# Queries and keys of the dilated mixer as 2x2 block products: seven products for eight, in a written order

## The chip, the cores and the metric

The kernel runs on one core of one Trainium2 chip. The metric is the device time of one execution in microseconds (us), the median of several runs. Engines are named as in the profile: PE (TensorE, matmul), PEld (its weight loads), DVE (VectorE), ACT (ScalarE), POOL (GpSimd) and SP (SyncE, which here issues every DMA). L12 is line 12 of the kernel.

## The reference

One layer of an encoder over 1024 tokens of width 1024, in float32. The input is normalised and multiplied by one wide matrix, whose columns feed two attention mixers, their gates and a merge:

```python
h = rmsnorm(x, attn_norm_g)
proj = h @ w_in
(c_q, c_kv, k_rope, z_mla, q_dil, k_dil, v_dil, z_dil, g_mla, g_dil) = jnp.split(proj, ...)
a_out = mla_attention(c_q, c_kv, k_rope, ...)              # 8 heads, dense
y_mla = (a_out * silu(z_mla)) @ w_o_mla
d_out = dilated_mixture(q_dil, k_dil, v_dil, positions)    # 24 heads of 64
y_dil = (d_out * silu(z_dil)) @ w_o_dil
merged = sigmoid(g_mla + b) * y_mla + sigmoid(g_dil + b) * y_dil
return x + merged @ w_out                                  # and a last rmsnorm
```

`dilated_mixture` applies rope (a rotation of the two halves of each head by cosine and sine tables) to `q_dil` and `k_dil`, then lets three groups g = 0, 1, 2 of 8 heads attend in windows with dilation 1, 4 and 16. The change concerns `q_dil` and `k_dil`: h times 3072 of the columns of `w_in`, then rope.

## The kernel before

**Numbers.** Every product is float32 out of three fast matmuls: an operand x is split into a high part (a cast by ACT, L75) and a low part x - high (a subtraction by POOL or DVE, L76), and `mm3` (L67 to L71) adds high·high, high·low and low·high in PSUM. The normalised input lies transposed in SBUF as hT_h and hT_l (8 blocks of 128 rows by 1024 tokens); its factor per token, R, is multiplied in later (for queries and keys it is folded into the rope tables cs_d).

**Stages on PE.** First the latent projections, the latents of mixer A and the dilated values (`dil_v`, six calls, one for each group g and half "quad" of its heads), to 229.6 us. Then `dil_qk` (L371 to L404), 12 items: for quad 0 and 1, for g = 0, 1, 2, for q and k. Then dilated attention (`dil_attention`, L724), dense attention (`mla_attention`, L499), and `output` (L796).

**One item of `dil_qk`.** It loads two weight tiles of 1024 x 128 (`wtile`, L79: load w_raw, cast w_h on ACT, subtract w_l on POOL), a for the first halves of four heads, b for the second. For each half of the tokens it makes two PSUM tiles, pa and pb, of 8 row blocks x 3 matmuls, 128x512 each: 96 matmuls an item. `rope` (L226) makes four DVE products out of each pair (L233), POOL subtracts and adds (L234, L235). For g < 2 the result is split again (ACT, POOL) into dq_st; for g = 2 ACT copies it in another token order (L397). The result goes to HBM (s_dq, s_dk) in DMAs of 32 rows, 128 KB each, from where attention loads it head by head: op_b the queries, op_a the keys, op_c the values.

**What sets the order.** The Tile scheduler orders every engine's instructions from the program, its dependences and its own estimates; pools of SBUF and PSUM tiles set when a tile may be written again. In the six-buffer PSUM pool pj of this stage, PE can work ahead of DVE. All DMAs go through SP's queue in order, so that one that waits holds up those behind it.

**At the stage's end.** `run` opens the PSUM pools of attention and starts `fillers` (L415): the 32 projections for z and the gates, 24 matmuls of 128x512 each half, that are fed between attention's steps (`feed`, L55). FIRST_FEED = 19 steps go ahead of the first scores (s_ps, L634). Scores pass `soft_block` (L603: on DVE L607, which needs the masks, on ACT L608). The masks are loaded into a pool that takes over SBUF from dil_qk's tiles. Attention's op tiles lie in SBUF that is free during `dil_qk`, and the first two heads' loads are issued inside that stage.

Of the kernel before, what the change touches and what calls it, by code (L numbers as in the profile page):

```python
# [39 lines left out]


# [8 lines left out]
class Net:  # L50
# [16 lines left out]
    def mm3(self, out, lh, ll, rh, rl, start, stop):  # L67
        mm = self.nc.tensor.matmul
        mm(out, lh, rh, start=start, stop=False)  # L69
        mm(out, lh, rl, start=False, stop=False)  # L70
        return mm(out, ll, rh, start=False, stop=stop)  # L71
# [7 lines left out]
    def wtile(self, src, wp=None, n=8):  # L79
        raw = self.wp.tile([128, 8, 128], F32, name="w_raw")  # L80
        wp = wp or self.wp
        h = wp.tile([128, 8, 128], F32R, name="w_h")
        l = wp.tile([128, 8, 128], F32R, name="w_l")
        self.dma(raw[:, :n], src)
        self.split(raw[:, :n], h[:, :n], l[:, :n], self.nc.gpsimd)
        return h, l

    def proj_half(self, w, half, pool):

        return run_all(self.proj_steps(w, half, pool))  # L90

    def proj_steps(self, w, half, pool):
# [3 lines left out]
        for kc in range(8):  # L96
            self.mm3(ps, w[0][:, kc], w[1][:, kc], self.hTh[:, kc, t], self.hTl[:, kc, t], kc == 0, kc == 7)
            if kc < 7:
                yield
# [235 lines left out]
    def dil_v(self, g, quad, tp, pj):  # L335
# [3 lines left out]
        for kk in range(2):  # L339
            raw = self.wp.tile([128, 4, 256], F32, name="w_raw")  # L340
            wp = (self.wp, self.wpx)[kk]
            h = wp.tile([128, 4, 256], F32R, name="w_h")
            l = wp.tile([128, 4, 256], F32R, name="w_l")
            self.dma(raw, a["wv"][g * 2 + quad, kk])
            self.split(raw, h, l, nc.gpsimd)
            w.append((h, l))
        for t in range(8):
            ps = pj.tile([128, 512], F32, name="pj")[:, :256]
            for kc in range(8):
                wh, wl = w[kc // 4]  # L350
                sl = slice(128 * t, 128 * t + 128)
                self.mm3(ps, self.hTh[:, kc, sl], self.hTl[:, kc, sl], wh[:, kc % 4], wl[:, kc % 4], kc == 0, kc == 7)
# [18 lines left out]
    def dil_qk(self, g, quad, which, tp, pj):  # L371

        nc, a = self.nc, self.a
        base = T_QK + (g * 2 + quad) * 4 + which * 2
        wa, wb = self.wtile(a["wt"][base]), self.wtile(a["wt"][base + 1], wp=self.wpx)
        if g < 2:
            st = [[tp.tile([128, S], F32R, name=f"dq_st{c}{p}") for p in range(2)] for c in range(2)]
        else:
            st = [[tp.tile([128, S], F32, name=f"dq_st{c}0")] for c in range(2)]
        for half in range(2):  # L380
            c512 = slice(half * 512, half * 512 + 512)
            pa, pb = self.proj_half(wa, half, pj), self.proj_half(wb, half, pj)
            o = self.rope(pa, pb, self.cos_d[:, c512], self.sin_d[:, c512], tp)
            for c in range(2):
                if g == 0:
                    self.split(o[c], st[c][0][:, c512], st[c][1][:, c512], nc.gpsimd)
                    continue
                if g == 1:
                    src = o[c].rearrange("p (m r) -> p r m", r=4)
                    dst = [x.rearrange("p (r m) -> p r m", r=4)[:, :, 128 * half:128 * half + 128] for x in st[c]]  # L390
                    self.split(src, dst[0], dst[1], nc.gpsimd)
                else:

                    src = o[c].rearrange("p (m b e) -> p e b m", b=8, e=2)
                    dst = st[c][0].rearrange("p (e b m) -> p e b m", e=2, b=8)[:, :, :, 32 * half:32 * half + 32]
                    for e in range(2):
                        nc.scalar.copy(out=dst[:, e], in_=src[:, e])  # L397
        off = 64 if (g == 0 and which) else 0
        dst = (self.dq if which == 0 else self.dk)[g]
        for c in range(2):  # L400
# [619 lines left out]
```

## Time and profile before

| what | value |
| --- | --- |
| runs | 1333.28, 1333.55, 1335.28 us; median 1333.55 |
| profiled execution | 1340.99 us, of which the span is 1339.2 us |
| granted PE clock, mean | 0.983 |
| values, latents (PE) | to 229.6 us |
| `dil_qk` (PE) | 229.67 to 490.9 us |
| dilated attention | about 498 to 835 us |
| dense attention | about 835 to 1200 us |
| output | to the end |

The profile counts from the start of the span. A row of groups reads: line, engine, operation, what is written <- what is read (names without buffer numbers), partitions x elements, how often | busy us, mean ns of one | idle time of the engine ahead of it, and who ended it. A timeline row starts with the start and the length in us; in brackets stands how long the engine was idle before and who ended that. "DMA to landing" is the time from issue to arrival.

### The profile page before, as it was taken

Reading aid. Unit: us, or ns where it says so; the run is one execution under the profiler, and the core shown is the slowest. Engines: PE = TensorE matmul, PEld = TensorE weight load, DVE = VectorE, ACT = ScalarE, POOL = GpSimd, SP = SyncE. Lnnn points to the kernel's source line nnn. Section 1 sums busy time; section 2 is a strip of 40 time slices with the busy share of each in tenths; the row PEclk is TensorE's granted clock in tenths of the full one; section 3 lists DMA queues with packets and bytes.
Section 4 is the critical chain, followed back from the end, with each engine's and each line's share of the span. In section 5 each row is a group of like instructions: output and inputs, shape, how many; then the busy total and the mean of one; then the engine's idle time right before and its main releaser. Section 6 shows DMA issues by size and latency. Waiting matters only on the chain.

```text
span 1339.2 us, 19315 instructions
## 1 busy us (share of the span) xinstructions
PE 1275.4 (95%) x7101; PEld 1108.4 (83%) x7101; DVE 655.4 (49%) x1204; ACT 563.3 (42%) x1102; POOL 455.0 (34%) x302
## 2 busy tenths in 40 slices
PE   8989999999999999988989889999999999998998
PEld 8879999888888878877878777788888878886786
DVE  7483520222222224656576565656555556558622
ACT  6533332123322225545455453455554545444322
POOL 2251212576466634525422031212111022035522
PEclk9989999999999999989999999999999999999999
DMA  9747562585345535678777778545333463136322
GB/s 322 227 154 272 196 248 80 162 217 159 106 115 151 135 98 164 163 184 224 190 186 208 196 195 203 156 120 160 92 99 100 103 178 119 63 116 205 131 96 75
DMA packets 128253, 213.03 MB, mean 159 GB/s; under 512 B 36440, under 2 KB 65696, under 8 KB 126304
## 3 DMA queue, kind: packets, MB, share of 16 engines
q1 hardware_dynamic: 128160, 211.81, 54.6%
q8 instruction: 56, 0.92, 0.3%
q14 instruction: 37, 0.30, 0.1%
HBM read 143.01 MB, written 68.75 MB: 158 GB/s over the span
## 4 chain that ended last, share of the span: by engine, by line
PE 70%; DMA 9%; DVE 5%; issue 2%; SPq 1%; ACT 1%; POOL 1%; DVEq 0%; ACTq 0%; POOLq 0%
PE pj L69 17%; PE pj L70 16%; PE pj L71 16%; PE pt L543 4%; PE av L552 2%; PE av L551 2%; PE s_mla L69 2%; PE s_mla L71 2%; PE s_mla L70 2%; DMA s_sd<-av_t 2%; PE pt L642 2%; SPq L65 1%; PE av L663 1%; DMA op_a<-s_dk 1%; PE s_ps L698 1%
## 5 line engine op out<-in xcount | busy, mean ns | idle before, releaser
L69 PE MATMUL pj<-hT_h,w_h 128*128 128x512 f32 x768 | 315.0, 410 | 3.7 <-DVE zg_z L428 2.1
L76 POOL TENSOR_TENSOR w_l<-w_raw,w_h 128x1024 fp32r<-128x1024 f32 (+1 forms) x70 | 167.5, 2396 | 441.1 <-ACT w_h L75 371.4
L71 PE MATMUL pj<-hT_h,w_l 128*128 128x512 f32 x768 | 301.9, 393 | 0.0
L70 PE MATMUL pj<-hT_l,w_h 128*128 128x512 f32 x768 | 301.6, 393 | 0.0
L233 DVE TENSOR_TENSOR rope_m<-pj,cs_d 128x512 f32<-128x512 f32 x96 | 61.9, 686 | 241.1 <-PE pj L71 241.1
L76 DVE TENSOR_TENSOR pt_l<-pt,pt_h 128x512 fp32r<-128x512 f32 x192 | 131.6, 686 | 89.0 <-ACT pt_h L75 87.1
L71 PEld LDWEIGHTS pj<-hT_h,w_l 128*128 128x128 f32 x768 | 145.3, 189 | 31.5
L69 PEld LDWEIGHTS pj<-hT_h,w_h 128*128 128x128 f32 x768 | 145.8, 190 | 29.7 <-DVE zg_z L428 3.0
L75 ACT CAST pt_h<-pt 128x512 fp32r<-128x512 f32 x192 | 112.0, 584 | 130.0 <-PE pt L543 60.0
L70 PEld LDWEIGHTS pj<-hT_l,w_h 128*128 128x128 f32 x768 | 146.0, 190 | 24.4
L70 PE MATMUL pj<-w_l,hT_h 128*128 128x256 f32 x384 | 109.6, 286 | 0.0
L71 PE MATMUL pj<-w_h,hT_l 128*128 128x256 f32 x384 | 109.4, 285 | 0.0
L69 PE MATMUL pj<-w_h,hT_h 128*128 128x256 f32 x384 | 109.3, 285 | 0.0
L75 ACT CAST w_h<-w_raw 128x1024 fp32r<-128x1024 f32 (+1 forms) x70 | 72.3, 1034 | 74.5 <-PE pj L70 59.5
L529 DVE TENSOR_REDUCE m_nm<-s_mla 128x1 f32<-128x1024 f32 x64 | 78.0, 1221 | 32.6 <-PE s_mla L71 32.4
L608 ACT ACTIVATE p<-p,d_st 128x256 f32<-128x256 f32 x128 | 64.4, 505 | 60.5 <-DVE d_st L607 60.4
L532 ACT ACTIVATE p<-s_mla,m_nm 128x1024 f32<-128x1024 f32 x64 | 71.8, 1123 | 25.5 <-PE pt L543 19.2
L543 PE MATMUL pt<-consts,p 128*128 128x128 f32 x512 | 79.6, 276 | 0.0
L552 PE MATMUL av<-pt_l,op_c 128*128 128x256 f32 x256 | 67.2, 286 | 8.5 <-DVE pt_l L76 8.5
L69 PEld LDWEIGHTS pj<-w_h,hT_h 128*128 128x128 f32 x384 | 73.6, 192 | 1.1
L607 DVE CUSTOM_DVE_ANT_0 p<-s_ps,masks 128x256 f32<-128x256 f32 x128 | 51.0, 417 | 48.0 <-PE s_ps L635 27.3
L70 PEld LDWEIGHTS pj<-w_l,hT_h 128*128 128x128 f32 x384 | 73.7, 192 | 0.7
(232 smaller groups left out, 2548.4 us busy)
## 6 DMA issues: line engine op xcount, KB each, us to landing
w_raw<-wt SPq DMA_DIRECT2D x48, 512.0 KB, 4.7
op_b<-s_dq SPq DMA_DIRECT2D x32, 512.0 KB, 8.5
s_dq<-dq_st SPq DMA_DIRECT2D x80, 128.0 KB, 2.6
s_dk<-dq_st SPq DMA_DIRECT2D x80, 128.0 KB, 2.4
gate<-s_gt SPq DMA_DIRECT2D x34, 256.0 KB, 3.0
s_dv<-dv_st SPq DMA_DIRECT2D x32, 256.0 KB, 3.9
s_gt<-zg_t SPq DMA_DIRECT2D x32, 256.0 KB, 3.7
w_raw<-wv SPq DMA_DIRECT2D x12, 512.0 KB, 5.9
```

The source lines that it names most:

```text
L69: mm(out, lh, rh, start=start, stop=False)
L70: mm(out, lh, rl, start=False, stop=False)
L71: return mm(out, ll, rh, start=False, stop=stop)
L75: self.nc.scalar.copy(out=h, in_=raw)
L76: sub.tensor_tensor(out=l, in0=raw, in1=h.bitcast(F32), op=ALU.subtract)
L233: v.tensor_tensor(out=mi, in0=p, in1=tab, op=ALU.mult)
L529: v.tensor_reduce(out=nm[:, hh, qb:qb + 1], in_=s, axis=AX.X, op=ALU.max, negate=True)
L532: nc.scalar.activation(out=p, in_=s, func=AF.Exp, bias=nm[:, hh, qb:qb + 1], accum_out=den[:, hh, qb:qb + 1])
L543: self.anchor = nc.tensor.transpose(pt[:, o:o + 128], P[b2][:, 128 * kc:128 * kc + 128], self.ident)
L552: nc.tensor.matmul(a_out, vv[:, kc], pl[:, s], start=False, stop=kc == 7)
L607: nc.vector.tensor_tensor_reduce(out=p, in0=s, in1=mask, op0=ALU.add, op1=ALU.min, scale=-0.125, scalar=3e38, accum_out=nm)
L608: nc.scalar.activation(out=p, in_=p, func=AF.Exp, scale=-1.0, bias=nm, accum_out=den)
```

## The change

`dil_qk` goes. An item is now computed as a product of 2x2 blocks in seven block products in place of eight (Strassen's method in Winograd's form). The weights' blocks are a or b by the upper or lower 512 rows; the activations' blocks are the first or second 512 tokens by the same rows. Each block product is 4 row blocks x 3 matmuls, 128x512.

- The activations' four sums (s0 to s3, high and low, 64 KB a partition) are made once (`block_sums`), beside the last four `dil_v`: x^T is loaded again, scaled on ACT, summed on POOL, split on ACT and DVE.
- Per item POOL makes four differences of weight blocks (`block_minus`) and the seven operands' low parts (`block_operand`), five places (LEAD) ahead of their products.
- The products gather in four PSUM banks a, b, c, d, of two sets in turn, so that all eight banks are used. ACT copies three of them, DVE adds these in place, and rope follows in place: sines into SBUF, cosines in the bank, then the difference and the sum, which POOL did before.
- All of this stands under `manual_schedule`: `blocks` writes the order of each engine, place by place.

```diff
+    def block_minus(self, j, items):
+        n, k = divmod(j, 7)
+        if n < len(items) and k in (2, 3, 4, 6):
+            b = self.blk[n]
+            out, x, y = {2: ((0, 0), (0, 1), (0, 0)), 3: ((0, 1), (1, 1), (0, 1)), 4: ((0, 0), (1, 1), (0, 0)), 6: ((1, 0), (1, 0), (0, 0))}[k]
+            self.nc.gpsimd.tensor_tensor(out=b[out], in0=b[x], in1=b[y], op=ALU.subtract)
...
+    def block_product(self, j, ps):
+        k = j % 7
+        hx = lambda i, c: tuple(x[:, 4 * c:4 * c + 4, 512 * i:512 * i + 512] for x in (self.hTh, self.hTl))
+        act = (lambda: hx(0, 0), lambda: hx(0, 1), lambda: self.s[0], lambda: self.s[2], lambda: self.s[1], lambda: self.s[3], lambda: hx(1, 1))[k]()
+        w = self.opd.pop(j)
+        out = ps["abcdacd"[k]]
+        for kc in range(4):
+            self.mm3(out, w[0][:, kc], w[1][:, kc], act[0][:, kc], act[1][:, kc], k < 4 and kc == 0, k in (1, 4, 5, 6) and kc == 3, skip=True)
...
+        steps = {
+            2: [lambda: copied(0, a)],
+            3: [lambda: add(b, 0)],
+            4: [lambda: copied(1, c)],
+            5: [both],
+            6: [lambda: copied(2, a), lambda: add(a, "t")],
+            7: [lambda: add(c, 2)],
+            9: [lambda: add(d, 2)],
+        }
...
+        r0, r1 = rope(0, b, c), rope(1, d, a)
+        put(7, r0[0])
+        put(8, r0[1])
+        put(8, r0[2])
+        put(9, r1[0])
+        put(10, lambda: high(0, (b, c)))
+        put(10, r1[1])
+        put(11, r1[2])
+        put(11, lambda: low(0, (b, c)))
+        put(12, lambda: high(1, (d, a)))
+        put(12, lambda: store(0))
+        put(12, lambda: low(1, (d, a)))
+        put(13, lambda: store(1))
...
+        with self.tc.manual_schedule():
+            for x in range(1, places + 14):
+                n, k = divmod(x - 1, 7)
+                j = x - 1
+                if j < places:
...
+                    self.block_product(j, ps[n])
+                todo = []
+                for m, y in ((n, k + 1), (n - 1, k + 8)):
+                    if m in steps:
+                        todo += steps[m].pop(y, [])
+                for f in todo:
+                    f()
+                self.block_operand(j + LEAD, items)
+                self.block_minus(j + LEAD + 1, items)
+                if k == 2 and n + 2 < len(items):
+                    self.block_loads(n + 2, items[n + 2])
```

Three edits go with it. **Stores by tile:** an item of g = 0 is stored in 4 DMAs, of g = 1 in 8, of g = 2 in 2, in place of 16, 16 and 8; s_dq and s_dk are laid out in HBM by quad and row for it. Attention then loads a head's keys in two DMAs, not one, and for g = 2 queries and keys in eight, not four. **Waits by bytes:** every pool gets `reuse_waits="tile"`, so that a tile waits for those tiles alone whose bytes it takes over. **Weights in pieces:** `wtile` and `dil_v` split weights in halves, each with tiles of its own.

```diff
-        self.dma(k[:, :S + pad], self.dk[g][h].rearrange("a c r t -> (a c r) t"))
+        for p in range(2):
+            self.dma(k[64 * p:64 * p + 64, :S + pad], self.dk[g][h // 4][:, hr, p])
...
-            with tc.tile_pool(name="op", bufs=1) as self.op, tc.tile_pool(name="ap", bufs=1) as ap:
+            with tc.tile_pool(name="op", reuse_waits="tile", bufs=1) as self.op, tc.tile_pool(name="ap", reuse_waits="tile", bufs=1) as ap:
```

How instructions stand is shown at three places. The first is DVE in the middle of the stage. Before (pj are the PSUM tiles pa and pb of one half, L233 rope's products):

```order
L233 TENSOR_TENSOR rope_m1_4257<-pj_4231,cs_d_544 128x512
L233 TENSOR_TENSOR rope_m2_4258<-pj_4231,cs_d_544 128x512
L233 TENSOR_TENSOR rope_m0_4320<-pj_4270,cs_d_544 128x512
L233 TENSOR_TENSOR rope_m3_4323<-pj_4270,cs_d_544 128x512
L233 TENSOR_TENSOR rope_m1_4321<-pj_4295,cs_d_544 128x512
L233 TENSOR_TENSOR rope_m2_4322<-pj_4295,cs_d_544 128x512
```

Now (st_a0 to st_d0 are one item's banks, st_a1 to st_d1 the next one's; st_c and st_t are SBUF copies; L450 and L451 combine, L483 to L491 are rope, L514 is the low part):

```order
L514 TENSOR_TENSOR dq_st00_3196<-st_b0_2968,dq_st00_3196 128x512
L514 TENSOR_TENSOR dq_st10_3197<-st_c0_2969,dq_st10_3197 128x512
L450 TENSOR_TENSOR st_t_3245<-st_d1_3138,st_c_3222 128x512
L514 TENSOR_TENSOR dq_st01_3247<-st_d0_2970,dq_st01_3247 128x512
L514 TENSOR_TENSOR dq_st11_3248<-st_a0_2967,dq_st11_3248 128x512
L451 TENSOR_TENSOR st_a1_3135<-st_a1_3135,st_t_3245 128x512
L451 TENSOR_TENSOR st_c1_3137<-st_c1_3137,st_c_3274 128x512
L483 TENSOR_TENSOR rope_m0_3299<-st_c1_3137,cs_d_543 128x512
L483 TENSOR_TENSOR rope_m1_3301<-st_b1_3136,cs_d_543 128x512
L487 TENSOR_TENSOR st_b1_3136<-st_b1_3136,cs_d_543 128x512
L487 TENSOR_TENSOR st_c1_3137<-st_c1_3137,cs_d_543 128x512
L490 TENSOR_TENSOR st_b1_3136<-st_b1_3136,rope_m0_3299 128x512
```

Where DVE only multiplied out of PSUM, it now combines, rotates and splits, with the ends of one item between the beginnings of the next, and many rows write the bank that they read.

The second place is DVE at the hand-over to attention. Before, the last rope products are followed by the first filler's z (L428) and the first soft_block (L607):

```order
L233 TENSOR_TENSOR rope_m1_4321<-pj_4295,cs_d_544 128x512
L233 TENSOR_TENSOR rope_m2_4322<-pj_4295,cs_d_544 128x512
L428 TENSOR_TENSOR zg_z_4386<-pj_4361,R_95 128x512
L607 ISA p_4469,d_st_4459<-s_ps_4468,masks_4453 128x256
L607 ISA d_st_4459 128x1
```

Now the same z (L601) and soft_block (L780) stand behind what the last product leaves to do:

```order
L451 TENSOR_TENSOR st_d1_4486<-st_d1_4486,st_c_4598 128x512
L483 TENSOR_TENSOR rope_m0_4625<-st_a1_4483,cs_d_543 128x512
L483 TENSOR_TENSOR rope_m1_4627<-st_d1_4486,cs_d_543 128x512
L487 TENSOR_TENSOR st_d1_4486<-st_d1_4486,cs_d_543 128x512
L487 TENSOR_TENSOR st_a1_4483<-st_a1_4483,cs_d_543 128x512
L490 TENSOR_TENSOR st_d1_4486<-st_d1_4486,rope_m0_4625 128x512
L491 TENSOR_TENSOR st_a1_4483<-st_a1_4483,rope_m1_4627 128x512
L601 TENSOR_TENSOR zg_z_4695<-pj_4670,R_95 128x512
L780 ISA p_4783,d_st_4772<-s_ps_4782,masks_4766 128x256
```

Seven operations on the last bank and its neighbour now stand between the last product and z, where two stood.

The third place is SP's queue around the masks' load. Before (s_dk_67 are the last item's stores; the first heads' loads of op_a, op_b and op_c stand some 60 rows earlier):

```order
L65 DMA s_dq_64<-dq_st_4055 32x1024 x4
L65 DMA w_raw<-wt 128x1024
L65 DMA s_dk_67<-dq_st_4204 32x1024 x4
L65 DMA s_dk_67<-dq_st_4205 32x1024 x4
L65 DMA masks<-masks 128x1280
```

Now:

```order
L67 DMA s_dq_64<-dq_st_4545 128x1024
L67 DMA op_b<-s_dq_62 64x1x2048 x2
L67 DMA op_a<-s_dk_65 64x1x1152 x2
L67 DMA op_c<-s_dv_68 128x9x128
L67 DMA op_b<-s_dq_62 64x1x2048 x2
L67 DMA op_a<-s_dk_65 64x1x1152 x2
L67 DMA op_c<-s_dv_68 128x9x128
L67 DMA w_raw<-wt 128x1024
L67 DMA s_dk_67<-dq_st_4629 128x1024
L67 DMA s_dk_67<-dq_st_4630 128x1024
L67 DMA masks<-masks 128x1280
```

The first two heads' loads have come behind the stage, between the last two items' stores: their SBUF is that of the sums.

More of the change, by code (lines that the diff above doesn't have):

```diff
@@ new lines, in run @@
+                            self.dil_v(0, 1, vp, pj)
+                    sp = sums.enter_context(tc.tile_pool(name="sums", reuse_waits="tile", bufs=1))
+                    with tc.tile_pool(name="bs", reuse_waits="tile", bufs=1) as tp:
+                        self.block_sums(sp, tp)
+                        self.dil_v(1, 0, vp, pj)
+                    for g, quad in ((1, 1), (2, 0), (2, 1)):
+                        self.dil_v(g, quad, vp, pj)
+                    for x in (self.cos_d, self.sin_d):
+                        for half in range(2):
+                            c = slice(512 * half, 512 * half + 512)
+                            nc.gpsimd.tensor_tensor(out=x[:, c], in0=x[:, c], in1=self.R[:, c], op=ALU.mult)
@@ L946, in run @@
             at.close()
-            with tc.tile_pool(name="yo", bufs=5, space=PSUM) as py:
+            with tc.tile_pool(name="yo", reuse_waits="tile", bufs=5, space=PSUM) as py:
                 self.output(py)
```

259 lines of the change are left out of this document (173 added, 86 removed).

## The prediction

> **What bounds the kernel now.** I read the page from the top: busy shares, the chain, the costliest groups.
>
> ```profile
> span 1339.2 us, 19315 instructions
> PE 1275.4 (95%) x7101; PEld 1108.4 (83%) x7101; DVE 655.4 (49%) x1204; ACT 563.3 (42%) x1102; POOL 455.0 (34%) x302
> PE 70%; DMA 9%; DVE 5%; issue 2%; SPq 1%; ACT 1%; POOL 1%; DVEq 0%; ACTq 0%; POOLq 0%
> L69 PE MATMUL pj<-hT_h,w_h 128*128 128x512 f32 x768 | 315.0, 410 | 3.7 <-DVE zg_z L428 2.1
> ```
>
> TensorE (PE) is busy for 95% of the span, so a matmul that goes is worth its pitch wherever PE never waits. Whether that holds in the changed stage is read from that stage's own windows. The columns are the stretch, its length, then busy time of PE, PEld, DVE, ACT and POOL with instructions, the granted clock, DMA share and GB/s:
>
> ```profile
> 250.00:300.00 50.00, 50.00 (x223) 41.39 (x221) 11.60 (x18) 12.35 (x14) 34.26 (x23) 1.00 0.75 206
> 300.00:350.00 50.00, 50.00 (x222) 41.42 (x221) 11.99 (x19) 14.60 (x17) 29.64 (x19) 1.00 0.57 155
> 350.00:400.00 50.00, 50.00 (x223) 41.39 (x222) 12.50 (x20) 13.76 (x19) 30.25 (x21) 1.00 0.38 106
> 400.00:450.00 50.00, 50.00 (x222) 41.42 (x221) 11.60 (x18) 13.62 (x14) 34.85 (x23) 1.00 0.50 137
> ```
>
> PE has no gap and the full clock; DVE is a quarter busy, ACT a quarter, POOL two thirds. So PE alone paces this stage, and the other engines have room, POOL least. The pitch is 200 us by 890 matmuls = 0.225 us. The whole stage gives it more exactly. These are its first and last matmul in the timeline, and the first of the next stage:
>
> ```profile
> 229.67 0.40 PE L69 MATMUL pj<-hT_h,w_h 128*128 128x512 f32 x1
> ...
> 490.62 0.39 PE L71 MATMUL pj<-hT_h,w_l 128*128 128x512 f32 x1
> ...
> 492.48 0.47 PE L69 MATMUL pj<-hT_h,w_h 128*128 128x512 f32 x1 [1.47 <-DVE rope_m L233]
> ```
>
> With 12 items of 96 matmuls, 1152 in all, that is 260.95 us over 1151 gaps = 0.2267 us.
>
> **What goes.** Seven products of 4 row blocks and 3 matmuls are 84 per item: 1008 in place of 1152, of the same form. 144 x 0.2267 = **32.6 us**, if PE stays the pace. An item then has 19.0 us, a product (a "place") 2.72 us.
>
> **What the other engines must do in 19.0 us.** Grouped rows of the stage, forms apart:
>
> ```profile
> L233 DVE TENSOR_TENSOR rope_m<-pj,cs_d 128x512 f32<-128x512 f32 x94 | 60.6, 686 | 237.1 <-PE pj L71 237.1
> L76 POOL TENSOR_TENSOR w_l<-w_raw,w_h 128x1024 fp32r<-128x1024 f32 x24 | 57.5, 2396 | 32.3 <-DMA s_dv<-dv_s 18.3 <-ACT w_h L75 14.1
> L76 POOL TENSOR_TENSOR dq_st<-rope_m,dq_st 128x512 fp32r<-128x512 f32 x32 | 45.0, 1431 | 0.0
> L235 POOL TENSOR_TENSOR rope_m<-rope_m,rope_m 128x512 f32<-128x512 f32 x23 | 29.8, 1295 | 0.0
> L75 ACT CAST dq_st<-rope_m 128x512 fp32r<-128x512 f32 x32 | 27.9, 872 | 91.7 <-POOL rope_m L234 53.9 <-POOL rope_m L235 24.5 <-DMA s_dk<-dq_st 6.6
> L75 ACT CAST w_h<-w_raw 128x1024 fp32r<-128x1024 f32 x23 | 24.3, 1055 | 54.3 <-PE pj L70 54.3
> L397 ACT COPY dq_st<-rope_m 128x256 f32<-128x256 f32 x28 | 16.6, 640 | 41.4 <-POOL rope_m L234 36.3 <-POOL rope_m L235 4.8
> L76 DVE TENSOR_TENSOR pt_l<-pt,pt_h 128x512 fp32r<-128x512 f32 x192 | 131.6, 686 | 89.0 <-ACT pt_h L75 87.1
> L75 ACT CAST pt_h<-pt 128x512 fp32r<-128x512 f32 x192 | 112.0, 584 | 130.0 <-PE pt L543 60.0
> ```
>
> *DVE*: 5 combines, 12 of rope, 4 low parts (none for g=2): 21 x 0.686 = 14.4 us, 76%. Each reads one PSUM and one SBUF operand, as the two DVE rows do. New is that most write their PSUM bank in place, which no row shows. I take 0.686 because inputs, shape and type are those of these rows; below, back to back, the pairs of L233 run at 0.645 (1.29 us for two). The point at which DVE takes over the pace is 19.0/21 = 0.905 us.
>
> *POOL*: 7 low parts of 128x512 at half of 2396 and 4 differences at 1.295 = 13.6 us; all eleven at 1.431 are 15.7 us, 83%. It takes over at 19.0/11 = 1.73 us.
>
> *ACT*: 3 copies out of PSUM at 0.584, 7 casts at half of 1055, 4 high parts at 0.872 (or 8 at 0.640): 8.9 to 10.6 us.
>
> So operands, made five places (13.6 us) ahead, and combines, with two places (5.4 us) until the item after next wants the bank, hide behind the products. If POOL or DVE ran 10% over 19.0 us, the stage would cost 12 x 1.9 = 23 us more. Rope's sums leave POOL for DVE; that is counted above. Stores fall from 160 to 56 DMAs; they lie under the products in both.
>
> The row that could speak against DVE at 0.686 is a DVE subtraction with both operands in SBUF, against L233 under the same busy POOL (min/median/max ns):
>
> ```profile
> L76 DVE TENSOR_TENSOR mg_l<-gate,m x16: 678/1251/1783, 1216.1 to 1254.3; 128x512 fp32r<-128x512 f32 x16
> L233 DVE TENSOR_TENSOR rope_m<-pj,cs_d x96: 680/688/694, 235.4 to 491.7; 128x512 f32<-128x512 f32 x96
> ```
>
> With two SBUF inputs the same shape stretches to 1251; with one in PSUM it never exceeds 694. The combines are of the second kind, so I keep 0.686. [...]
>
> **The block sums** are new: 16 reloads of x^T, 16 ACT scalings, 16 POOL sums, 16 splits (ACT cast, DVE subtract). SP issues the reloads behind the last latents' stores and the first two stores of the fifth group of values, so some 40 us of value products (16 tiles of 24 matmuls at 0.12 us, less two tiles) still lie over them.
>
> ```profile
> 229.43 0.28 PE L70 MATMUL pj<-w_l,hT_h 128*128 128x256 f32 x1
> 229.55 0.28 PE L71 MATMUL pj<-w_h,hT_l 128*128 128x256 f32 x1
> w_raw<-wt SPq DMA_DIRECT2D x48, 512.0 KB, 4.7
> ```
>
> POOL needs 16 x 1.295 + 8 x 1.25 = 31 us, DVE 16 x 1.251 = 20 us beside it; the third product, the first that reads a sum, comes 5.4 us later still. About 14 us spare. The loads of item 1's weights, though, stand on SP behind a load for item 2, which waits for POOL's last operand of item 0, some 8 us into the stage; they land at 8 + 4.7, and POOL must then make an operand by 19 us. That fits, with POOL behind. For both I take **+1 us**, from 0 to 8.
>
> **The hand-over to attention** is where something comes back. T0 is the end of the last product (before: 490.62 + 0.23 = 490.85).
>
> ```profile
> 491.05 1.29 DVE L233 TENSOR_TENSOR rope_m<-pj,cs_d 128x512 f32<-128x512 f32 x2 [4.05 <-PE pj L71]
> ...
> 494.40 3.58 SPq L65 DMA_DIRECT2D s_dk<-dq_st  x8
> ...
> 500.27 0.35 SPq L65 DMA_DIRECT2D masks<-masks  x1
> ...
> 505.33 0.08 DVE L607 DVE_READ_ACCUMULATOR2_ANT d_st<- 128x1 f32 x1
> ...
> 505.47 0.39 PE L634 MATMUL s_ps<-op_a,op_b 128*128 128x256 f32 x1 [0.74 <-DVE d_st L607]
> ```
> ```profile
> DMA to landing us min/median/max: 3.9/3.9/3.9
> ```
>
> (The last row is the mask load's.) Before, soft_block waits for the masks, the masks for the last s_dk stores, whose SBUF they take; PE goes on at T0 + 14.6. After: DVE's 14 operations since the last but one product (7 from T0 - 2.7, 7 from T0) end at T0 + 6.5, ACT's four half copies at T0 + 9.1, two store issues (0.45 each) at T0 + 10, the masks' issue 2.3 later as before, landing 3.9 later, the first soft_block 0.8 and s_ps 0.5 behind: T0 + 17.5, **+2.9 us**. Meanwhile the scores' banks are the last item's accumulators: PE has 24 filler matmuls (to T0 + 5.4) and then stands 3.7 us until ACT has copied. In before PE stood 1.5 there. What so long a gap does is seen at a load wait:
>
> ```profile
> 574.00:578.60 4.60, 0.53 (x3) 0.13 (x1) 1.06 (x2) 1.29 (x3) 2.52 (x2) 0.92 1.04 261
> 578.60:580.00 1.40, 1.26 (x6) 1.29 (x7) 0.46 (x3) 0.00 (x0) 0.00 (x0) 0.50 0.99 205
> 584.00:588.00 4.00, 4.00 (x12) 3.23 (x12) 1.48 (x3) 0.31 (x1) 0.00 (x0) 0.50 0.84 254
> 588.00:592.00 4.00, 4.00 (x24) 3.42 (x23) 2.60 (x11) 2.24 (x9) 0.00 (x0) 0.98 0.21 16
> ```
>
> After some 4 us without matmuls the granted clock is 0.50 for about 9 us, which loses 4.7 us of work. At the hand-over PE must do 8 score and 24 filler matmuls (1 + 5.4 us) from T0 + 9.1: done at T0 + 15.5 at full clock, at T0 + 20.2 with those 4.7 us. So the hand-over costs from +2.9 to +5.6 us; I take **+4.3**. [...]
>
> The first two heads' loads, issued under the stage before, now wait for the sums' SBUF and start about T0 - 5 (the second sum's product is over at T0 - 5.4): 2.2 MB a head at 261 GB/s are 8.4 us, landed at T0 + 3.5, before the scores.
>
> **Elsewhere** keys come in two loads, class loads in eight, at 0.45 us of SP each; waits go by bytes. PE's waits that this touches, and the one it could shorten:
>
> ```profile
> PE pj L69 <- DVE gate L825: 5.3, 4, 2.1
> PE s_ps L634 <- DMA op_b<-s_dq: 4.2, 1, 4.2
> PE s_ps L634 <- DMA op_a<-s_dk: 3.3, 1, 3.3
> ```
>
> 12.8 us in all: from -5 to +8, taken as 0, since loads get later by a few issues and releases earlier.
>
> **The sum.** -32.6 + 1 + 4.3 = -27.3 us. The profiled execution took 1340.99 us (span 1339.2), so it would take 1313.7. It is 7.4 us over the median of the runs, 1333.55, at the same instructions; the stage ran at full clock there, so the difference carries over: **1306.2 us**. With both ends of the terms: 1333.55 - 32.6 + (0 to 8) + (2.9 to 5.6) + (-5 to +8) = 1298.9 to 1322.6.
>
> **Rivals.**
> - *DVE or POOL paces the stage, slower than before.* Place: DVE's in-place operations. It decides from 0.905 us an operation; the whole gain is gone when an item takes 19.0 + 27.3/12 = 21.3 us, at 1.01 us. With the 1.251 of the row with two SBUF inputs, 12 x (26.3 - 19.0) = 88 us less the 27.3: about 1394 us. For it: writes to PSUM by DVE are unseen. Against: 680 to 694 ns at PSUM inputs, under a POOL as busy as it will be. 7%.
> - *The hand-over or the start is dearer*: scores that wait for heads' loads crowded with the stores, item 1's weights late, sums late: 8 to 15 us more than taken, as a load wait with its half clock costs (4.2 + 4.7 us each): 1314 to 1322. For it: ten loads move from under the stage to its end. 15%.
> - *Waits by bytes gain besides*: the output stage's gate waits and head loads shorten by 5 to 9 us of those 12.8: 1297 to 1301. Against: most of these waits are for loads, not for releases. 8%.
> - *The gain is given back* in attention, by queues on SP that now hold more loads ahead of PE: within 2.7 us of 1333.55. It would take three more such load waits. 3%.
>
> **How the numbers follow.** The forecast holds 67%. Low 1297 takes in the third rival, high 1322 the second: some 88% by these cases, and I leave it so wide for what a new order in attention may do. A difference of 0.2% (2.7 us) is about what a measurement tells from none: faster 0.89, same 0.04, slower 0.07.
>
> **What would show it.** Right: 1008 block matmuls at 0.227 us without gaps, a stage near 229 us, DVE about 75% and POOL about 72 to 83% busy there, DVE operations near 0.69; a PE stop near 3.7 us after the first filler product, scores going on about T0 + 18 to 20. Wrong: PE waiting on w_l, st or sums inside the stage; in-place DVE operations over 0.9 us; attention longer by more than 8 us.

## The result

The changed kernel takes **1735.68 us** (median of 4 runs, 1733.21 to 1739.72) against 1333.41 us for the kernel before in the same comparison: a ratio of **1.3011, 95% interval 1.2978 to 1.3043**. It is slower by 30%, where the prediction had 1306.2 us in a range of 1297 to 1322 and gave "slower" 7 in 100. In the comparisons below one run of the version that loads the second head later took 4692.85 us and one of the kernel before 1400.65; the ratios leave both out, and their cause is not known.

### The profile page after: what moved, and what is told of

Read it like the earlier page. It is cut to its first block, busy times and chain, and to the rows that moved or that the text cites. A ratio compares the mean times of both kernels' runs of the same rounds, so it can differ in the third digit from the quotient of the medians.

```text
span 1733.7 us, 19520 instructions
## 1 busy us (share of the span) xinstructions
PE 1274.6 (74%) x6957; PEld 1105.9 (64%) x6957; DVE 752.8 (43%) x1359; ACT 610.6 (35%) x1276; POOL 498.5 (29%) x393
## 4 chain that ended last, share of the span: by engine, by line
PE 50%; DMA 29%; SPq 9%; DVE 6%; issue 3%; ACT 2%; POOL 1%; ACTq 0%; DVEq 0%; POOLq 0%
DMA op_a<-s_dk 13%; SPq L67 9%; PE pj L71 7%; PE pj L73 7%; PE pj L72 7%; DMA op_b<-s_dq 3%; PE pt L716 3%; DMA s_sd<-av_t 3%; DMA s_rr<-c_w 2%; PE av L725 2%; PE av L724 2%; PE s_mla L71 1%; PE s_mla L73 1%; PE s_mla L72 1%; PE st_a L73 1%
## 5 line engine op out<-in xcount | busy, mean ns | idle before, releaser
L78 POOL TENSOR_TENSOR w_l<-w_raw,w_h 128x512 fp32r<-128x512 f32 (+1 forms) x176 | 233.3, 1333 | 630.0 <-ACT w_h L77 534.6
L809 PE MATMUL s_ps<-op_a,op_b 128*128 128x256 f32 x128 | 47.2, 377 | 405.3 <-DMA op_a<-s_dk 244.4
L780 DVE CUSTOM_DVE_ANT_0 p<-s_ps,masks 128x256 f32<-128x256 f32 x128 | 51.8, 417 | 397.5 <-PE s_ps L810 273.5
L71 PE MATMUL pj<-hT_h,w_h 128*128 128x512 f32 x384 | 171.7, 447 | 1.9 <-DVE zg_z L601 1.9
L72 PE MATMUL pj<-hT_l,w_h 128*128 128x512 f32 x384 | 157.0, 409 | 0.0
L73 PE MATMUL pj<-hT_h,w_l 128*128 128x512 f32 x384 | 156.2, 407 | 0.0
L77 ACT CAST w_h<-w_raw 128x512 fp32r<-128x512 f32 (+1 forms) x176 | 106.0, 614 | 127.8 <-POOL w_raw L415 65.4
L73 PEld LDWEIGHTS pj<-hT_h,w_l 128*128 128x128 f32 x384 | 76.2, 198 | 17.8
L71 PEld LDWEIGHTS pj<-hT_h,w_h 128*128 128x128 f32 x384 | 77.7, 202 | 12.9 <-DVE zg_z L601 2.5
L72 PEld LDWEIGHTS pj<-hT_l,w_h 128*128 128x128 f32 x384 | 77.8, 203 | 10.3
L73 PEld LDWEIGHTS pj<-w_h,hT_l 128*128 128x128 f32 x384 | 73.4, 191 | 0.9
```

What stands on the lines that cost most here:

```text
L71: mm(out, lh, rh, start=start, stop=False, skip_group_check=skip)
L72: mm(out, lh, rl, start=False, stop=False, skip_group_check=skip)
L73: return mm(out, ll, rh, start=False, stop=stop, skip_group_check=skip)
L77: self.nc.scalar.copy(out=h, in_=raw)
L78: sub.tensor_tensor(out=l, in0=raw, in1=h.bitcast(F32), op=ALU.subtract)
L780: nc.vector.tensor_tensor_reduce(out=p, in0=s, in1=mask, op0=ALU.add, op1=ALU.min, scale=-0.125, scalar=3e38, accum_out=nm)
```

## The profile after

The page of the changed kernel: span, busy time, the granted clock in 40 slices, and the group with the longest idle time before it.

```profile
span 1733.7 us, 19520 instructions
PE 1274.6 (74%) x6957; PEld 1105.9 (64%) x6957; DVE 752.8 (43%) x1359; ACT 610.6 (35%) x1276; POOL 498.5 (29%) x393
PE   7999999999724443534634372355999999999998
PEclk9999999999956776666866785677999999999999
PE 50%; DMA 29%; SPq 9%; DVE 6%; issue 3%; ACT 2%; POOL 1%; ACTq 0%; DVEq 0%; POOLq 0%
...
L809 PE MATMUL s_ps<-op_a,op_b 128*128 128x256 f32 x128 | 47.2, 377 | 405.3 <-DMA op_a<-s_dk 244.4
```

PE is busy 74% of the span, not 95%. What is lost lies in one stretch, slices 12 to 28, and ahead of one group: the dilated scores, which wait 405.3 us. In the chain, DMA has gone from 9% to 29% and SP's queue from 1% to 9%.

**The stage that the change rewrites did what was forecast.** Windows in its middle, with the columns of the prediction's:

```profile
250.00:300.00 50.00, 50.00 (x217) 40.56 (x216) 32.72 (x53) 20.92 (x38) 36.08 (x29) 1.00 0.55 180
300.00:350.00 50.00, 50.00 (x218) 40.69 (x217) 31.34 (x52) 20.34 (x42) 36.71 (x30) 1.00 0.41 126
350.00:400.00 50.00, 50.00 (x218) 40.53 (x217) 30.54 (x50) 19.54 (x37) 35.62 (x29) 1.00 0.45 158
400.00:450.00 50.00, 50.00 (x219) 40.66 (x218) 34.05 (x56) 21.42 (x43) 36.26 (x29) 1.00 0.47 134
```

PE has no gap; DVE is busy 64%, POOL 72%. Its first and last products, and the operations whose price no row had shown:

```profile
L71 PE MATMUL st_a<-hT_h,w_h x48: 389/389/628, 224.8 to 442.1; 128*128 128x512 f32 x48
...
L451 DVE TENSOR_TENSOR st_a<-st_a,st_t x12: 699/700/700, 241.2 to 454.8; 128x512 f32<-128x512 f32 x12
...
L487 DVE TENSOR_TENSOR st_a<-st_a,cs_d x12: 685/689/691, 252.9 to 463.7; 128x512 f32<-128x512 f32 x12
```
```profile
L73 PE MATMUL st_d<-hT_h,w_l x48: 387/389/389, 243.7 to 459.3; 128*128 128x512 f32 x48
```

The stage lasts from 224.8 to 459.3 + 0.2, that is 234.7 us, where it was 261.2: 26.5 us less. DVE in place in PSUM takes 0.69 to 0.70 us.

**The loads of attention are what broke.** Who PE waited for (us in total, times, longest):

```profile
PE s_ps L809 <- DMA op_a<-s_dk: 244.4, 10, 29.5
PE s_ps L809 <- DMA op_b<-s_dq: 80.6, 3, 28.0
PE s_ps L809 <- issue: 43.7, 2, 24.1
PE s_ps L809 <- DVE d_st L780: 36.6, 3, 35.2
```

Before, op_a and op_b cost 3.3 and 4.2 us. How such a load runs is seen where nothing else does. Three windows, the last two with PE idle (the last three columns are granted clock, DMA share and GB/s), and SP's timeline from the stage's end:

```profile
454.00:462.00 8.00, 8.00 (x37) 6.52 (x36) 5.73 (x10) 2.37 (x6) 1.30 (x1) 1.00 0.13 40
...
470.00:480.00 10.00, 0.00 (x0) 0.00 (x0) 0.00 (x0) 0.00 (x0) 0.00 (x0) 0.50 0.13 52
...
574.00:582.00 8.00, 0.00 (x0) 0.00 (x0) 0.00 (x0) 0.00 (x0) 0.00 (x0) 0.50 0.13 51
```
```profile
463.30 24.41 SPq L67 DMA_DIRECT2D op_b<-s_dq  x2
487.81 10.52 SPq L67 DMA_DIRECT2D op_a<-s_dk  x2
498.38 9.54 SPq L67 DMA_DIRECT2D op_c<-s_dv  x1
508.04 13.16 SPq L67 DMA_DIRECT2D w_raw<-wt  x1
521.30 1.11 SPq L67 DMA_DIRECT2D s_dk<-dq_st  x2
530.17 0.33 SPq L67 DMA_DIRECT2D masks<-masks  x1
```

A DMA share of 0.13 is 2 of 16 engines (0.125), and 40 to 52 GB/s are 20 to 26 GB/s for each. The packets in the trace say the same: from 470 to 480 us two are under way at any time (three for 3% of it), where in the kernel before it is 16 or more from 574 to 582 us, where PE waits for a load too. SP needs 24.41 us to issue two DMAs, for 1.92 at 450.71; what holds it, the trace does not show. All that stands behind on SP is late with them: the values, the filler's weight, the last key stores, the masks. PE stands long and often here, and the granted clock is 0.5 to 0.8 in the slices of this stretch, 0.50 in the two windows with PE idle (0.865 over the whole execution).

Why two engines? In the new HBM layout a head's queries are two blocks of 32 rows, one for each rope half, with the other three heads' rows between them. The transfer's outermost loop has two entries. Before, both halves followed one another and made one loop of 64 rows. The trace shows the two engines and not their reason; that it is the two entries of the loop is my guess, and the runs below test it.

## The experiments

The **theory**: the loads are slow since their outer loop of two runs on two engines. **Rival 1**: the loads are late, since the order on SP and the waits by bytes put them behind other work. **Rival 2**: the longer contiguous runs (8 KB) are slow. Each run has its own comparison with the kernel before; times are set against that.

### Four runs on the cause

**The loads in blocks of 32 rows.**

```diff
-        for rows in (slice(0, 64), slice(64, 128)):
-            self.dma(q[rows], self.dq[g][h // 4][:, hr])
-        for p in range(2):
-            self.dma(k[64 * p:64 * p + 64, :S + pad], self.dk[g][h // 4][:, hr, p])
+        for r in range(0, 128, 32):
+            self.dma(q[r:r + 32], self.dq[g][h // 4][r // 32 % 2, hr])
+        for r in range(0, 128, 32):
+            self.dma(k[r:r + 32, :S + pad], self.dk[g][h // 4][r // 32 % 2, hr, r // 64])
```

> The changed kernel, but queries and keys of g = 0 and 1 are loaded in DMAs of 32 rows (one for each rope half), not of two times 32: 9 DMAs a head instead of 5, each with one row loop of 32. Theory (a transfer whose outer loop has two entries runs on two of the 16 DMA engines): the loads spread again, attention falls from 750 to about 335 to 360 us, the time to 1300 to 1335, and the waits of the scores on op_a and op_b from 325 us to under 40. Rival 1 (the loads are late since SP's order and the waits by bytes put them behind other work): the same waits and four more issues a head, so the time stays over 1650. Rival 2 (runs of 8 KB are slow): these DMAs have runs of 8 KB too, so it stays over 1600.

Measured: 1324.57 us, ratio **0.9912 (0.9878 to 0.9946)**. Twice the DMAs for the same bytes, and 411 us are gone. The scores' waits on op_b have fallen from 80.6 us to the 5.8 below, those on op_a from 244.4 to 0.5:

```profile
PE s_ps L809 <- DMA op_b<-s_dq: 5.8, 3, 2.8
```

**The halves of a row side by side.** The layout is (quad, row, half, part, token), so that 32 rows x 2 halves are one loop of 64. Stores, keys and the loads of g = 2 follow it in the same way and are left out here.

```diff
-            self.dq = [dt(f"s_dq{g}", (2, 2, 128, 2 if g < 2 else 1, S), ...
+            self.dq = [dt(f"s_dq{g}", (2, 128, 2, 2 if g < 2 else 1, S), ...
...
-            self.dma(q[rows], self.dq[g][h // 4][:, hr])
+            self.dma(q[rows], self.dq[g][h // 4][hr].rearrange("r c p t -> (r c) p t"))
```

> The changed kernel with the two rope halves of a row side by side in HBM, so that a head's queries (and keys of one part) are one loop of 64 rows: as many DMAs in attention as the changed kernel, fewer for g = 2. The order of rows within a head's contraction changes in the same way for queries and keys. Theory (two engines): 1298 to 1330 us, at or below the run with 32 rows, as SP issues less. Rival 1 (order, waits by bytes): over 1650. Rival 2 (8 KB runs): over 1600.

Measured: 1323.99 us, ratio **0.9913 (0.9880 to 0.9947)**, the same as with 32 rows, with the size and number of the changed kernel's loads (fewer for g = 2). So it is the loop that costs, not the size of a load nor the number of SP's issues.

**The kernel before with the layout, the stores and the loads alone.**

```diff
-                for j in range(4):
-                    self.dma(dst[quad * 4 + j, p, c, :, off:off + S], st[c][p][32 * j:32 * j + 32])
+                self.dma(dst[c, :, p, off:off + S], st[c][p])
...
-            self.dma(q[rows], self.dq[g][h].rearrange("p c r t -> (c r) p t"))
+            self.dma(q[rows], self.dq[g][h // 4][:, hr])
...
```

> The kernel before with nothing of the block products and no waits by bytes: only the new layout of queries and keys in HBM, the stores of whole tiles, and the changed kernel's loads. Theory (two engines): attention grows by about 400 us as in the changed kernel, 1690 to 1800 us, with stretches of DMA share near 0.125. Rival 1 (order by hand and waits by bytes): neither is there, 1315 to 1350 us. Rival 2 (8 KB runs): slower, by the wait on op_b alone, 1400 to 1500.

Measured, in one run: 1731.36 us beside 1335.26, 396 us more, without a block product, a written order or a wait by bytes. PE's waits there:

```profile
PE s_ps L634 <- DMA op_a<-s_dk: 249.5, 9, 30.7
PE s_ps L634 <- DMA op_b<-s_dq: 78.8, 3, 28.2
```

The two sums are within 6 us of the changed kernel's 244.4 and 80.6. Rival 1 falls.

**The queries part by part**, runs of 4 KB.

```diff
-            self.dma(q[rows], self.dq[g][h // 4][:, hr])
+            for p in range(2):
+                self.dma(q[rows, p], self.dq[g][h // 4][:, hr, p])
```

> The changed kernel with a head's queries loaded part by part: twice the DMAs, runs of 4 KB in place of 8, the outer loop still of two entries. Theory (two engines): no gain, 1690 to 1800 us. Rival 2 (8 KB runs): the waits on op_b go, and with them at least 80 us: under 1650. Rival 1: no gain either, or some loss.

Measured, in one run: 1717.58 us, 18 us less than the changed kernel, where rival 2 asked for at least 80. It falls too; the 32-row runs with their 8 KB had already spoken against it.

### Half of the fault

**The queries alone spread** (32 rows), the keys as in the changed kernel.

> The changed kernel with the queries alone spread (DMAs of 32 rows); the keys keep their loops of two times 32. Theory (two engines, 53 GB/s for both together, as the stretches with nothing else show): queries and keys, 16 heads of 1.0 + 0.55 MB, need 25 MB / 53 GB/s = 470 us at least on two engines, the keys alone 8.8 MB / 53 = 165 us, which fits under an attention of 335 us but makes each pair of key loads last 10 us: 1330 to 1420 us, with waits on op_a and few on op_b. Rival (any load with a loop of two stalls SP's queue as a whole): over 1550.

Measured: 1483.15 us, ratio 1.1111 (1.1069 to 1.1153). It lies between, as the theory has it, but 63 us over the range that I gave. What I had left out stands in this run's timeline of SP:

```profile
589.26 17.84 SPq L67 DMA_DIRECT2D op_b<-s_dq  x8
```

Eight loads of 32 rows, which the theory spreads over all engines, take 17.84 us to issue; at 514.24 in the same run four such took 1.72. Two loads of keys had been issued at 581.69, and from 594 to 596 us the DMA share is 0.13. What stops SP there is not shown, and no run tests it by itself. The rival's stop of SP's queue is thus there in part. The spread queries are late too: PE waits 62.4 us on op_a here and still 44.7 on op_b, for 5.8 with both in 32 rows.

### What was left of the gain

With the loads mended the forecast's other terms can be read. The row-pairs run gains 0.9%, the prediction's 27.3 us were 2.0%. These are points in time of its profiled execution beside those of the kernel before. The two executions took 1315.2 and 1340.99 us; the one is 8.8 us under the median of its runs, the other 7.4 over. So the column adds up to -25.8 us where the medians in one comparison differ by 11.3: it shows where time went, and the ratios show how much.

| stretch | before, us | row pairs, us | change |
| --- | --- | --- | --- |
| to the stage's first product | 229.67 | 227.02 | -2.7 |
| stage, to T0 (end of the last product) | 261.2 | 234.7 | -26.5 |
| T0 to the scores behind the first soft_block | 14.6 | 24.5 | +9.9 |
| from there to the first s_mla | 317.2 | 319.2 | +2.0 |
| to the first product of w_out | 420.7 | 412.7 | -8.0 |
| to the end | 95.8 | 95.3 | -0.5 |

The -8.0 us of dense attention (the last row but one) seem to go for the most part with the waits by bytes. In one profiled execution of each, this stretch takes 412.2 to 415.6 us in the four versions of this document with spread loads, these waits and the masks in their old pool. It takes 419.1 in the version without these waits, and 417.0 in the kernel before when they are given to it alone.

The hand-over costs twice what was forecast. Its timeline in the row-pairs run (T0 is 461.7), and three windows:

```profile
469.79 1.67 SPq L67 DMA_DIRECT2D s_dk<-dq_st  x2
481.74 0.33 SPq L67 DMA_DIRECT2D masks<-masks  x1
```
```profile
486.25 0.58 PE L809 MATMUL s_ps<-op_a,op_b 128*128 128x256 f32 x1 [11.06 <-DVE d_st L780]
```
```profile
452.00:462.00 10.00, 10.00 (x45) 8.09 (x44) 4.21 (x7) 2.31 (x5) 2.59 (x2) 1.00 0.98 272
462.00:472.00 10.00, 8.82 (x43) 7.15 (x42) 6.35 (x11) 4.41 (x10) 0.00 (x0) 1.00 1.06 224
472.00:482.00 10.00, 3.19 (x15) 2.30 (x13) 0.00 (x0) 0.62 (x1) 0.01 (x1) 0.76 0.85 251
```

For 30 us the DMA engines are all but full: they move 7.5 MB, 4.4 of them two heads' loads. The last key stores stand behind these, so that the masks, which take over the stores' SBUF, are issued 10.3 us after the last store's issue, not 2.3; the scores go on at T0 + 24.5. Ahead of that PE stood 1.18 us for ACT's copies behind the first filler product, not the 3.7 of the sum: a half copy took 0.37 to 0.42 us where 0.640 was assumed.

**Masks first**, in a pool over the sums' SBUF. Attention's pool `ap` is opened anew for dense attention, to make room.

```diff
-            with tc.tile_pool(name="op", ...) as self.op, tc.tile_pool(name="ap", ...) as ap:
-                with tc.tile_pool(name="dx", ...) as dx, ...
-                    m = dx.tile([128, 1280], F32, name="masks")
+            with tc.tile_pool(name="op", ...) as self.op:
+                with tc.tile_pool(name="mk", ...) as mk, tc.tile_pool(name="ap", ...) as ap, tc.tile_pool(name="dx", ...) as dx, ...
+                    m = mk.tile([128, 1280], F32, name="masks")
...
+                with tc.tile_pool(name="ap2", ...) as ap, tc.tile_pool(name="brd", ...) as bp, ...
```

> The run with row pairs, with the masks in a pool over the sums' SBUF in place of the one over the stage's own tiles, so that their load stands ahead of the first heads' loads and waits for no store. (Attention's small pool is opened anew for dense attention, to make room.) In the row-pairs run PE stood 11.06 us at the hand-over for the first soft_block, and the granted clock fell. Theory (the masks wait for the last key stores, which stand in the DMA rings behind 4.4 MB of heads' loads): that wait falls below 3 us and the kernel gains 9 to 14 us against the row-pairs run of the same chip. Rival (the heads' loads themselves are late, the masks only hide it): the scores then wait for op_a or op_b in its place, and the gain is under 4 us.

Measured: 1341.75 us, ratio **1.0047 (1.0028 to 1.0066)**: a miss, and in two ways. The wait for the masks went, but two waits for op_a came (2.44 and 6.98 us), as the rival had it. And the new pool brought a stop of its own, which the edit was not meant to have (timelines of PE, POOL and ACT):

```profile
842.77 1.26 POOL L968 TENSOR_TENSOR num<-num 128x512 f32<-128x512 f32 x1 [0.69 <-DVE num L966]
844.06 2.36 DVE L702 TENSOR_REDUCE m_nm<-s_mla 128x1 f32<-128x1024 f32 x2 [1.44 <-POOL num L968]
845.38 1.11 ACT L705 ACTIVATE p<-s_mla,m_nm 128x1024 f32<-128x1024 f32 x1 [19.42 <-DVE m_nm L702]
```
```profile
846.64 0.69 PE L716 MATMUL pt<-consts,p 128*128 128x128 f32 x2 [27.97 <-ACT p L705]
```

Dense attention's first tiles, by the waits in these rows, now lie over `num` of the last pair and wait until POOL has combined it: DVE's maximum starts behind POOL, ACT behind DVE, and PE stands for 27.97 us.

**Masks first and other banks.** In the row-pairs run PE stood at its first block product:

```profile
225.98 0.62 ACT L77 CAST s_h<-y 128x512 fp32r<-128x512 f32 x1 [3.60 <-POOL y L398]
226.50 0.47 ACT L376 ACTIVATE dv_s<-pj,rcol 128x256 f32<-128x256 f32 x1
```
```profile
227.02 0.50 PE L71 MATMUL st_a<-hT_h,w_h 128*128 128x512 f32 x1 [3.25 <-ACT dv_s L376]
```

Its bank was still to be copied out by ACT, and ACT stood behind a sum on POOL. Here the first item's a and b get banks that are free for long.

```diff
-                        ps[n] = {c: pp.tile([128, 512], F32, name=f"st_{c}{n % 2}") for c in "abcd"}
+                        ps[n] = {c: pp.tile([128, 512], F32, name=f"st_{c}{n % 2}") for c in ("cdab", "bcda")[n % 2]}
```

> The run with the masks first, and the PSUM banks dealt in another order: the first item's first two products get banks that the value products left long ago, and the last item's banks that are finished first are those that the first scores take. At the stage's start PE stood 3.25 us for ACT's copy out of the last but one value tile (ACT waited for a sum on POOL), and ran at half clock for some 3 us after it. Theory (the bank is what it waits for): the stop goes, 3 to 6 us less than the masks-first run. Rival (the first operands or the sums are late too): the stop moves to w_l or s_h at the first or third product, and less than 2 us is gained.

Measured: 1338.20 us, ratio 1.0019 (0.9999 to 1.0039), 3.6 us under the masks-first run by the medians, though the two intervals overlap. The stop at the first product is gone and the first product stands at 222.93; 1.56 us of it come back at the sixth product, which waits for ACT's copy of bank c.

**The banks alone**, without the masks' pool.

> The run with row pairs and, of the run with masks first, only the other order of the PSUM banks; the masks and attention's pools stay as in the changed kernel. There the stop of 3.25 us at the stage's start went and the stage began and ended about 4 us earlier. Theory: the same here, a ratio to the kernel before 0.3 points under the row-pairs run's 0.9913 (0.985 to 0.990), without the stop of 27 us that dense attention had in the masks-first runs. Rival (that stop came with the banks): it is here too, and the ratio is 1.00 or more.

Measured: 1320.33 us, ratio **0.9882 (0.9846 to 0.9919)**; no stop in dense attention, so it was the masks' pool that brought it. The interval overlaps the row-pairs run's, so the 0.3 points rest on the points in time more than on the times. At the hand-over the stop is as long as ever, 11.64 us.

**The second head's loads behind the masks** (with the banks).

```diff
+        later = ExitStack()
+        if g == 0 and h == 1:
+            later.enter_context(self.tc.issue_after(self.mask_dma.ins))
         for rows in (slice(0, 64), slice(64, 128)):
             self.dma(q[rows], ...)
...
+        later.close()
```

> As the run with the banks, and the second head's loads are issued behind the masks' load (an order on SP only). The last key stores and the masks then have 2.2 MB of heads' loads ahead of them in the rings, not 4.4. Theory (the masks wait for the stores, the stores for the rings): the wait of 11 us for the first soft_block falls to 3 to 5 us, and the kernel gains 5 to 9 us against the run with the banks, ratio 0.979 to 0.985. Rival (the bandwidth of the heads' loads decides, in whatever order): the scores of the second head wait instead, and the two runs are equal within 2 us.

Measured: **1311.06 us, ratio 0.9814 (0.9790 to 0.9838)** by five of six runs, the fastest version that computes the layer, 1.9% under the kernel before. SP and PE at its hand-over (T0 is 457.16):

```profile
463.31 0.92 SPq L67 DMA_DIRECT2D s_dk<-dq_st  x2
467.67 0.33 SPq L67 DMA_DIRECT2D masks<-masks  x1
468.10 1.09 SPq L67 DMA_DIRECT2D op_b<-s_dq  x2
```
```profile
472.86 0.39 PE L813 MATMUL s_ps<-op_a,op_b 128*128 128x256 f32 x1 [2.46 <-DVE d_st L780]
```

Against the banks alone the stop has fallen from 11.64 to 2.46 us, and the scores go on at T0 + 15.7. Its rival falls: the second head waits 1.52 us.

**Waits by bytes, taken away and given alone.** First the row-pairs run without them, in every pool (`reuse_waits="tile"` taken out):

> The run with row pairs without waits by bytes: pools wait as in the kernel before. If waits by bytes gain in the output stage and at pool edges as the prediction's third rival has it, this is 5 to 9 us slower than the row-pairs run, 1325 to 1335; if block sums and the block stage lean on them, more than 15 us slower, with PE waiting at the stage's start; if they do nothing, equal within 3 us.

Measured: 1337.85 us, ratio 1.0017 (1.0000 to 1.0035), one point over the row-pairs run and between the first two cases of the expectation. The stage starts with a stop of 7.3 us and the hand-over has two, of 6.6 and 7.3; dense attention is 6.4 us longer too (419.1 for 412.7). Then the kernel before with them:

> The kernel before, with waits by bytes in every pool and nothing else. Without them the row-pairs run lost 14 us (6.62 us at the hand-over, 4 us at the stage's start, more after). If waits by bytes gain mostly at the edges that the block products made (sums and their operands over other tiles), this is within 5 us of the kernel before, either way; if they gain by themselves, it is 10 to 14 us faster, and the block products' own part of the gain is none.

Measured: 1332.02 us, ratio 0.9973 (0.9951 to 0.9996). Alone they gain 0.3%; for the block products they are what keeps the stage's edges and the later stages from eating the whole gain.

**Products on hT in place of the sums.** The stage has 234.7 us where 1008 matmuls at 0.2267 make 228.5. This run leaves the sums out as operands (they are still made), so its output is not the layer's.

```diff
-        act = (lambda: hx(0, 0), lambda: hx(0, 1), lambda: self.s[0], lambda: self.s[2], lambda: self.s[1], lambda: self.s[3], lambda: hx(1, 1))[k]()
+        act = (lambda: hx(0, 0), lambda: hx(0, 1), lambda: hx(0, 0), lambda: hx(0, 1), lambda: hx(1, 0), lambda: hx(0, 0), lambda: hx(1, 1))[k]()
```

> The run with row pairs, with the four products that read the activations' sums reading blocks of hT instead: it leaves out the sums as operands (they are still made). In the row-pairs run matmuls on hT into banks a and b go at 0.2267 us as before, those on the sums at 0.2335. If reading the sums' tiles costs the 3%, all products go at 0.227 and the stage is 4 to 5 us shorter; if it is the banks or what runs beside (DVE and ACT reading and writing PSUM), the four products stay at 0.2335.

Measured, in one run: the stage goes from 227.62 to 457.85, 230.2 us, 4.5 us less, and products into every bank run alike. Groups of it (busy us, mean ns of one, idle time before):

```profile
L71 PE MATMUL st_c<-hT_h,w_h 128*128 128x512 f32 x84 | 32.7, 389 | 0.0
L71 PE MATMUL st_d<-hT_h,w_h 128*128 128x512 f32 x84 | 32.7, 389 | 0.0
```

The same banks in the row-pairs run, and one product of it from its first matmul to the next product's:

```profile
L71 PE MATMUL st_c<-s_h,w_h 128*128 128x512 f32 x84 | 33.1, 394 | 0.0
L71 PE MATMUL st_d<-hT_h,w_h 128*128 128x512 f32 x41 | 16.1, 394 | 0.0
```
```profile
300.84 0.39 PE L71 MATMUL st_c<-s_h,w_h 128*128 128x512 f32 x1
...
303.64 0.40 PE L71 MATMUL st_d<-hT_h,w_h 128*128 128x512 f32 x1
```

Twelve matmuls on a sum take 2.80 us, 0.233 each for 0.2267. It hangs on the sums' being read, not on the banks nor on what runs beside. The product on hT that follows them is slower too (394 for 389), so it isn't simply a matter of those tiles; the mechanism stays open. The run took 1306.45 us as a whole, beside 1336.43. Without a reader the sums' SBUF is free early: the first two heads' queries and keys are issued at 265.83 and 287.33 us, inside the stage as before, and PE waits 1.47 us for the first soft_block.

## Why the prediction was wrong

- **The step that failed** is the one headed "Elsewhere": "keys come in two loads, class loads in eight, at 0.45 us of SP each ... from -5 to +8, taken as 0". It costed the new loads by their number and SP's issues and never by the loop that they run over. They cost about 400 us: 396 when given alone to the kernel before, 411 taken from the changed kernel. The number of loads, which I did weigh, cost nothing: 1324.57 us with nine a head, 1323.99 with five.
- With it fell "2.2 MB a head at 261 GB/s": that rate was one of the old loads, with another shape. It did not carry over: these loads ran at 40 to 52 GB/s.
- None of the four rivals held this. "The hand-over or the start is dearer" priced late loads at 4.2 + 4.7 us each, as a wait seen before, and the range ended there. "The gain is given back" looked at the right place, attention's loads on SP, but asked for three such waits and had 3 in 100.
- **The saving** was right in kind: 144 matmuls less, PE never waiting inside the stage, 26.5 us for the forecast 32.6. The rest is 4.5 us for reading the sums, by one execution of each, and about 2 us that go with the half clock behind the stop at the start (0.50 from 225.93 to 229.34 us in the changed kernel, half of 3.41 us).
- **DVE, POOL and ACT** had room, as forecast: DVE took 0.69 to 0.70 us in place for the assumed 0.686, far from 0.905 and from the 1.251 at which 21 operations would make 26.3 us an item, and POOL 1.295. They were busy 64% and 72% for 76% and 72 to 83%, ACT 41% for 47 to 56%. The first rival is refuted.
- **The start** was +1 us in a range of 0 to 8. PE stood there, 2.19 us in the changed kernel and 3.25 in the row-pairs run, but through ACT's copy of a value tile behind POOL's sums, which the text did not name. Even so the stage began earlier than before, at 224.81 and 227.02 us for 229.67. Without waits by bytes it began at 233.11, so they are what made it earlier.
- **The hand-over** was mis-sized: +2.9 to +5.6 forecast, +9.9 measured once the loads are spread. The failing term is "the masks' issue 2.3 later as before": the stores then had the DMA engines to themselves and landed 2.1 us after their issue, now they stand behind the heads' loads and land after 10.6 (row-pairs run). With one head less in front, the scores go on at T0 + 15.7, under the T0 + 17.5 of the sum at full clock. PE's stop behind the filler was priced too dear, 3.7 us for 1.18.
- **Waits by bytes** were weighed as a small gain in the output stage; they are worth about one point to this version, at the stage's start and end and in dense attention. The third rival had the kind of gain right, and its place not: the output stage stayed as it was (95.3 us for 95.8).

The forecast was 2.0%. The two versions that mend this step alone gain 0.9%, some 11 of the 27.3 us by the medians, so the sum would have been too high without it as well. By the two traces 6 us at the products and 6 at the hand-over were lost that it had not counted, and most of that came back by gains at the start and in dense attention that it had not counted either. That the traces add up to 25.8 us, close to the sum, is thus luck in two ways: in errors that cancel, and in which executions were profiled. The 1.9% of the fastest version come with two further edits.

## What to carry to other kernels

When a layout in HBM changes, read each load and each store against the new strides: which loops merge, and how many entries the outermost one has left in HBM; bytes and counts of DMAs do not show it (1735.68 us here with a loop of two, 1323.99 with one of 64 in loads of the same size, fewer only for g = 2). A change of layout that was meant for the stores was paid at the loads here, and a steady DMA share of 0.13, two engines of sixteen, with PE idle was its mark in this profile. What stands behind a heavy load in the DMA queues (stores, a small table that all wait for) is part of that load's price: the masks went out 10.3 us after the last store behind two heads' loads, 2.3 before.

## What the runs showed of the hardware

- Loads with an outer loop of two ran on two DMA engines (share 0.13, two packets under way) at 40 to 52 GB/s, 20 to 26 GB/s for each engine, and runs of 4 KB in place of 8 in the queries changed little (1717.58 us for 1735.68).
- While such loads were under way, SP's issue stood still: 24.41 us for two of them, for 1.92 at 450.71, and 17.84 us for eight loads in blocks of 32 rows, where four took 1.72 at 514.24. The reason is not shown.
- A matmul of the same shape was 3% slower (0.233 for 0.2267 us) in products on the sums' tiles than in those on hT; the cause is open.
- DVE reading a PSUM bank and an SBUF tile and writing the same bank took 0.69 to 0.70 us for 128x512, as when it writes to SBUF (0.68 to 0.69).
